# Seven-product stage of a decoder trunk: partial sums written into PSUM banks by ScalarE, no root on normed tiles, and the query rope in one piece

## The chip, the core and the metric

The kernel runs on one core of a Trainium2 chip. Its time is device microseconds for one execution. A core has five engines that work through queues of their own in program order and wait for each other by semaphores: TensorE (PE in the profile; PEld is its weight load), VectorE (DVE), ScalarE (ACT), GpSimd (POOL) and SyncE (SP). SP and POOL issue most of the DMAs here.

## The reference, cut to what matters

A trunk of two layers on a sequence of 1024 tokens with a width of 1024, all in float32. The first layer is a gated linear recurrence, which the change does not touch. The second is latent attention with 8 heads. Between them lie the projections that concern us:

```python
h = rms_norm(x_stream, norm_kv)
ckr = h @ w_dkv                                    # 256 + 64 columns
c_kv = rms_norm(ckr[..., :KV_RANK], kv_norm)
k_rope = apply_rope(ckr[..., KV_RANK:], cos[None], sin[None])
...
h = rms_norm(x, norm_g)
u = h @ w_in                                       # 384 + 1024 columns
c_q = rms_norm(u[..., :Q_RANK], q_norm)
gate = u[..., Q_RANK:]
q = jnp.einsum("bsc,chd->bshd", c_q, w_uq)
q_rope = apply_rope(q[..., QK_NOPE:], cos[None, :, None], sin[None, :, None])
o = causal_block_attention(q_nope, q_rope, k_nope, k_rope, v)
y = o.reshape(bsz, seq, N_HEADS * V_DIM) * jax.nn.silu(gate)
```

with `rms_norm(x, g) = x * rsqrt(mean(x * x) + EPS) * g`. The 256 columns of c_kv and the 384 of c_q are normed a second time; the key's rope part and the gates are not.

## The kernel before

Data is kept transposed: 128 features on the partitions, tokens along the free axis, in pages of 1024 tokens and halves of 512. A float32 product is three matmuls (`mm3`, lines 113 to 116): each factor is split into a high part (`hl`, line 82, ScalarE's copy) and a low part (line 83, VectorE's difference), and hi·hi, hi·lo and lo·hi are added up in one PSUM bank.

First come the recurrence and its output projection, which leaves x1, the residual stream, as eight tiles. Its sum of squares is collected in `acc1` (`sq_a`), and `factors` makes seven combinations of the tiles, `fx[0]` to `fx[6]`: x1 times the joined projection (14 row blocks of 128) is done in seven pairs of row blocks by a scheme of seven products in the place of eight. `pair(m, dst, w, banks, mid)` does one pair (m = 0, 2, ... 12): each product is `fmul`, 12 matmuls on one `fx[i]` and one combination of weights from `wpair`, and four banks a, c, b, d take the products. Below, "product fx3" is the one on `fx[3]`.

In `pair` before, a, c, b and d take the products fx0 to fx3. ScalarE copies a to q1 (line 607); VectorE makes v2 = b - q1, u3 = d + v2 and, after `mid`, u3 - c. Then fx4 is added onto a, fx5 onto d, fx6 onto c, and VectorE adds or subtracts v2 for two of the results. Each of the four results is multiplied by `r1`, the root of x1 (`byr`, line 162).

Pair 0 gives the two tiles of c_kv (`kvt`), pair 2 the key's rope tile and the first tile of c_q (`qt`), pair 4 the other two, and the pairs 6, 8, 10 and 12 (loop at line 743, j = 0, 2, 4, 6) the gates. `mid` puts other work between the products: in pair 0 `roots` (the root of x1: sum over the partitions by a matmul on tiles of `acc1` split in two, lines 142 to 144, then `newton`, lines 148 to 151); in pair 2 `normed` for c_kv and in pair 6 `normed` for c_q (sums by the matmuls of line 661, then `newton`, then the multiplications of line 665). After pair 6 the tiles of c_q are split; after pair 8 `qrope(0)` and after pair 10 `qrope(1)` make the queries' rope parts: 36 matmuls each, then for each half six VectorE operations (lines 733 to 735) and two splits, whose results go to DRAM. Pair 12 takes its banks from the pool of the attention stage, which opens at line 750 when the pool of the earlier banks is closed.

`wpair` loads four weight blocks (SP; line 503, tile wa), multiplies each by its gain (line 507, four pieces on ScalarE), and makes seven combinations (line 519, VectorE), each split in a wh (ScalarE) and a wl (VectorE). There are four wh and four wl buffers: the split for a product waits until an earlier product has released one. Tiles named tk come from one pool of eight.

The order of instructions on each engine is set by a scheduler when the kernel is built, from the order of the code, priorities (`tc.high_priority`, weights ahead of the rest) and the release of buffers. On the chip each queue then runs in that order.

Of the kernel before, what the change touches and what calls it, by code (L numbers as in the profile page):

```python
# [9 lines left out]
F32 = mybir.dt.float32  # L10
F32R = mybir.dt.float32r
AF = mybir.ActivationFunctionType
ALU = mybir.AluOpType
# [5 lines left out]
D = 1024  # L19
NKT = 8  # L20
NCT = 10
NH = 8
EPS = 1e-6
SCALE = 192 ** -0.5
NEG = -1e30
P = 128
# [15 lines left out]
HW = 512  # L42
# [12 lines left out]
NA, CW, CB, BR, BI, LAM, NKV, KVN, NB, QN, FN, NVEC = 0, 8, 48, 58, 68, 78, 88, 96, 98, 106, 109, 117  # L55


def trunk(tc, xT, wina, vecs, wgate, wouta, winc, wuk, wuv, wuq, wuqr, woutb, rope, outT):
    nc = tc.nc
    V, A, T, G = nc.vector, nc.scalar, nc.tensor, nc.gpsimd  # L60
# [10 lines left out]
    def nm(s):  # L71
        uid[0] += 1
        return f"{s}_{uid[0]}"

    def page(dt=F32R):
        return pgs.tile([P, S], dt, tag="pg", name=nm("pg"))
# [46 lines left out]
    def hs(h):  # L123
        return slice(h * HW, (h + 1) * HW)
# [21 lines left out]

    def newton(out, ps, inv, y, u):
        A.activation(out=y, in_=ps, func=AF.Abs_reciprocal_sqrt, scale=inv)
        V.tensor_tensor(out=u, in0=y, in1=y, op=ALU.mult)
        V.scalar_tensor_tensor(out=u, in0=ps, scalar=inv, in1=u, op0=ALU.mult, op1=ALU.mult)  # L150
        V.scalar_tensor_tensor(out=out, in0=u, scalar=-3.0, in1=y, op0=ALU.add, op1=ALU.mult)

    def sumsq(acc, sq, first, n):

        if first:
            V.scalar_tensor_tensor(out=acc, in0=acc, scalar=EPS * n / P, in1=sq, op0=ALU.add, op1=ALU.add)
        else:
            V.tensor_tensor(out=acc, in0=acc, in1=sq, op=ALU.add)

    def byr(out, src, r):  # L160

        V.scalar_tensor_tensor(out=out, in0=src, scalar=-0.5, in1=r, op0=ALU.mult, op1=ALU.mult)
# [254 lines left out]
    for ct in range(NCT):  # L417
        ps = ps0[:2] if ct == 0 else psn
# [37 lines left out]
    acc1 = rbp.tile([P, S], F32, tag="rb", bufs=1, name="acc1")  # L456
# [45 lines left out]
    def wblock(m, h, t):  # L502
        nc.sync.dma_start(out=t, in_=winc[m, :, hs(h)])
        g = gkv if m < 3 else gb
        for k in range(4):
            c = slice(k * P, (k + 1) * P)
            A.activation(out=t[:, c], in_=t[:, c], func=AF.Copy, scale=g[:, 4 * h + k:4 * h + k + 1])
        return t

    def wpair(m, new):  # L510

        def split(t):
            hi = wp.tile([P, HW], F32R, tag="wh", bufs=4, name=nm("wh"))
            lo = wp.tile([P, HW], F32R, tag="wl", bufs=4, name=nm("wl"))
            hl(t, hi, lo)
            out.append((hi, lo))

        def add(o, x, y):
            V.tensor_tensor(out=o, in0=x, in1=y, op=ALU.add)

        out = []
        with tc.high_priority(offset=WPC):
            a11, a21, a22 = wblock(m, 0, new()), wblock(m + 1, 0, new()), wblock(m + 1, 1, new())
            split(a11)
            s = wp.tile([P, HW], F32, tag="wr", bufs=2, name=nm("ws"))
            add(s, a21, a22)
            split(s)
            add(s, s, a11)
            split(s)
            add(a11, a11, a21)  # L530
            split(a11)
            a12 = wblock(m, 1, new())
            split(a12)
            split(a22)
            add(a12, a12, s)
            split(a12)
        return out

    w1 = wtile(wouta[4], NCT)
# [11 lines left out]
    for j in range(1, 3):  # L551
        x1s = []
        for dt in (j, j + 4):
            xr = residual(dt)
            w = wtile(wouta[dt], NCT)
# [21 lines left out]
    w0 = wpair(0, tt)  # L577
# [7 lines left out]
    tcp = pc.enter_context(tc.tile_pool(name="tcp", bufs=1, reuse_waits="tile"))  # L585
    r1 = acc1

    def tmp(tag, dt=F32):
        return tcp.tile([P, HW], dt, tag=tag, name=nm(tag))

    def tk(dt=F32):
        return tcp.tile([P, HW], dt, tag="t", bufs=8, name=nm("tk"))

    def fmul(ps, w, i, js, first):
        for j in js:
            c = slice(j * P, (j + 1) * P)
            hi, lo = fx[i][j // 2]
            mm3(ps, (w[0][:, c], w[1][:, c]), (hi[:, hs(j % 2)], lo[:, hs(j % 2)]), first and j == 0, j == 3, not first)

    def pair(m, dst, w, banks, mid=None):  # L600

        a, c, b, d = banks
        q1, v2, u3 = tmp("q1"), tcp.tile([P, HW], F32, tag="v2", bufs=2, name=nm("v2")), tmp("u3")
        for i, ps in enumerate((a, c, b, d)):
            fmul(ps, w[i], i, range(4), True)
            if i == 0:
                A.activation(out=q1, in_=a, func=AF.Copy)
            elif i == 2:
                V.tensor_tensor(out=v2, in0=b, in1=q1, op=ALU.subtract)
            elif i == 3:  # L610
                V.tensor_tensor(out=u3, in0=d, in1=v2, op=ALU.add)
        if mid:
            mid()
        V.tensor_tensor(out=dst[1][1], in0=u3, in1=c, op=ALU.subtract)
        byr(dst[1][1], dst[1][1], r1[:, hs(1)])
        fmul(a, w[4], 4, range(4), False)
        byr(dst[0][0], a, r1[:, hs(0)])
        fmul(d, w[5], 5, range(4), False)
        V.tensor_tensor(out=dst[1][0], in0=d, in1=v2, op=ALU.add)
        byr(dst[1][0], dst[1][0], r1[:, hs(0)])  # L620
        fmul(c, w[6], 6, range(4), False)
        V.tensor_tensor(out=dst[0][1], in0=c, in1=v2, op=ALU.subtract)
        byr(dst[0][1], dst[0][1], r1[:, hs(1)])

    def wa():
        return tcp.tile([P, HW], F32, tag="wa", bufs=NWA, name=nm("wa"))
# [1 line left out]
    def four():  # L628
        return [pst() for _ in range(4)]

    def halves(t):
        return [t[:, hs(0)], t[:, hs(1)]]

    def square(ts, acc, j):
        for h in range(2):
            if j == 0:
                A.activation(out=acc[h], in_=ts[j][:, hs(h)], func=AF.Square)
            else:
                sq = tk()
                A.activation(out=sq, in_=ts[j][:, hs(h)], func=AF.Square)  # L640
                sumsq(acc[h], sq, j == 1, P * len(ts))

    def two():
        return tk(F32R), tk(F32R)
# [9 lines left out]
    def normed(ts, acc, ps_, gcol, fac):  # L654
        n = len(ts)
        gs = con.tile([P, n], F32, name=nm("gs"))
        V.tensor_scalar(out=gs, in0=vec[:, gcol:gcol + n], scalar1=-0.5 * fac, scalar2=None, op0=ALU.mult)
        for h in range(2):
            ps = pst()
            for i in range(2):  # L660
                T.matmul(out=ps, lhsT=onesr, rhs=ps_[h][i], start=i == 0, stop=i == 1)
            newton(acc[h], ps, 1.0 / (P * n), tk(), tk())
            for j in range(n):
                t = ts[j][:, hs(h)]
                V.scalar_tensor_tensor(out=t, in0=t, scalar=gs[:, j:j + 1], in1=acc[h], op0=ALU.mult, op1=ALU.mult)

    def roots():
        for h in range(2):
            rstd(acc1[:, hs(h)], r1[:, hs(h)], pst(), 1.0 / D, tk(), tk(), two())

    kvt = [page(F32) for _ in range(2)]
    kvacc = [tk() for _ in range(2)]
    pair(0, [halves(t) for t in kvt], w0, four(), roots)
    for j in range(2):
        square(kvt, kvacc, j)
    kvps = presum(kvacc)
    krt = page(F32)
    qt = [page(F32) for _ in range(3)]
    pair(2, [halves(krt), halves(qt[0])], wpair(2, wa), four(), lambda: normed(kvt, kvacc, kvps, KVN, 1.0))
    qacc = [tk() for _ in range(2)]  # L680
    square(qt, qacc, 0)


# [24 lines left out]
    for j in range(4):  # L708
        i = j ^ 1
        DQ.dma_start(out=krs[32 * j:32 * j + 32, :], in_=krt[32 * i:32 * i + 32, :])  # L710
    pair(4, [halves(qt[1]), halves(qt[2])], wpair(4, wa), four())
    for j in range(1, 3):
        square(qt, qacc, j)
    qps = presum(qacc)
# [28 lines left out]
    for j in range(0, NH, 2):  # L743
        gts = [[tk(), tk()] for _ in range(2)]
        w = wpair(6 + j, wa)
        if j < NH - 2:
            banks = four()
        else:

            pp.close()  # L750
            pss = es.enter_context(tc.tile_pool(name="pss", bufs=2, space=PSUM, reuse_waits="tile"))
            banks = [pss.tile([P, HW], F32, tag="pm", bufs=4, name=nm("pm")) for _ in range(4)]
        pair(6 + j, gts, w, banks, None if j else lambda: normed(qt, qacc, qps, QN, SCALE))
        for i in range(2):
            for h in range(2):
                A.activation(out=gts[i][h], in_=gts[i][h], func=AF.Silu)
                DQ.dma_start(out=gd[j + i, :, hs(h)], in_=gts[i][h])
        if j == 0:
            cq = []
            for t in qt:  # L760
                cq.append((page(), page()))
                for h in range(2):
                    hl(t[:, hs(h)], cq[-1][0][:, hs(h)], cq[-1][1][:, hs(h)])
            cs, sn = tables()
        elif j < NH - 2:
            qrope(j // 2 - 1)

    def pm():
        return pss.tile([P, HW], F32, tag="pm", bufs=4, name=nm("pm"))
# [323 lines left out]
```

## Time and profile before

| | |
|---|---|
| median of 3 runs | 898.17 us (896.16 to 898.38) |
| the profiled execution | 899.38 us, of which the span from first to last instruction is 897.6 |
| mean granted TensorE clock | 0.986 |
| busy in the span | TensorE 865.4, VectorE 685.1, ScalarE 498.6, GpSimd 80.3 us |
| seven-product stage | from 371.0 us (first product of pair 0), with the last pair from 519.4 us |

In a row of waits stands who waited, at which line and for which tile, for whom, with the sum, the number and the longest in us. A row of a timeline has the start, the duration (matmuls overlap, so the distance between two starts is their pace), the engine, the line, the operation, and in brackets the idle time ahead of it and what ended it. The granted clock is 1.00 when TensorE runs at full speed.

### The profile page before, as it was taken

To read this page: it belongs to the slowest core of one execution; us is meant where nothing else is said; L and a number is where in the kernel's file an instruction comes from. 1 tells how busy PE (TensorE), PEld (TensorE's weight loads), DVE (VectorE), ACT (ScalarE), POOL (GpSimd) and SP (SyncE) were. 2 spreads that over 40 slices of the span, in tenths; PEclk is the share of its full clock that TensorE was granted. 3 is DMA by queue.
4 is the path that set the end of the run, shared out by engine and by line. 5 is a ranking of instruction groups with operands and counts; after the bars stand their busy time and mean duration, and the time that the engine had idled before them with its cause. 6 is when DMAs were issued, how large, how long until landed. Compare 5 with 4: busy or idle time off the path is not lost. (4 is left out here: it accounts for less than half of the span.)

```text
span 897.6 us, 12180 instructions
## 1 busy us (share of the span) xinstructions
PE 865.4 (96%) x4326; PEld 732.8 (82%) x4326; DVE 685.1 (76%) x1260; ACT 498.6 (56%) x915; POOL 80.3 (9%) x147
## 2 busy tenths in 40 slices
PE   7999999999999999999999788999999999999995
PEld 5788888888887888878778567989989998888995
DVE  7888788777877754899999945878978887875453
ACT  6357776777787434596675324655655554431112
POOL 2111100111000100001211220000000000010000
PEclk9999999999999999999999989999999999999998
DMA  7333333333212544133435465222223235756032
GB/s 246 120 95 96 93 103 98 100 105 95 71 47 84 169 141 147 48 107 123 168 124 184 147 233 148 68 79 89 89 74 110 71 106 192 254 199 223 8 138 68
DMA packets 51789, 109.00 MB, mean 121 GB/s; under 512 B 6544, under 2 KB 16656, under 8 KB 51728
## 3 DMA queue, kind: packets, MB, share of 16 engines
q1 hardware_dynamic: 36240, 67.45, 23.4%
q0 software_dynamic: 15216, 40.51, 13.5%
q8 instruction: 34, 0.56, 0.3%
q10 hardware_dynamic: 272, 0.26, 0.1%
q14 instruction: 27, 0.22, 0.1%
HBM read 81.46 MB, written 26.21 MB: 120 GB/s over the span
## 5 line engine op out<-in xcount | busy, mean ns | idle before, releaser
L115 PE MATMUL ps<-pg,wh 128*128 128x512 f32 x672 | 262.5, 392 | 3.4 <-DVE pg L262 3.3
L114 PE MATMUL ps<-pg,wh 128*128 128x512 f32 x672 | 262.5, 393 | 1.9 <-ACT wh L82 1.1
L116 PE MATMUL ps<-pg,wl 128*128 128x512 f32 x672 | 262.3, 391 | 0.1
L115 PEld LDWEIGHTS ps<-pg,wh 128*128 128x128 f32 x672 | 126.9, 189 | 31.6 <-DVE pg L262 4.4
L114 PEld LDWEIGHTS ps<-pg,wh 128*128 128x128 f32 x672 | 126.5, 189 | 30.3 <-ACT wh L82 2.3
L116 PEld LDWEIGHTS ps<-pg,wl 128*128 128x128 f32 x672 | 126.8, 189 | 27.3 <-DVE wl L83 1.4
L82 ACT ACTIVATE pt<-pm 128x512 fp32r<-128x512 f32 (+2 forms) x96 | 44.4, 490 | 59.7 <-PE pm L856 56.0
L846 ACT ACTIVATE pg<-s,m 128x128 f32<-128x128 f32 (+3 forms) x64 | 47.5, 742 | 44.6 <-DVE m L843 39.8
L114 PE MATMUL pm<-pg,pg 128*128 128x256 f32 (+1 forms) x192 | 61.9, 322 | 0.0
L115 PE MATMUL pm<-pg,pg 128*128 128x256 f32 (+1 forms) x192 | 61.6, 321 | 0.0
L116 PE MATMUL pm<-pg,pg 128*128 128x256 f32 (+1 forms) x192 | 61.3, 319 | 0.0
L114 PE MATMUL pm<-pg,wh 128*128 128x512 f32 x108 | 43.4, 402 | 9.9 <-DVE tk L734 9.9
L83 DVE TENSOR_TENSOR pt<-pm,pt 128x512 fp32r<-128x512 f32 (+2 forms) x96 | 50.5, 547 | 1.9 <-ACT pt L82 1.8
L843 DVE TENSOR_REDUCE m<-s 128x1 f32<-128x128 f32 (+3 forms) x64 | 48.1, 753 | 1.0
L358 DVE SCALAR_TENSOR_TENSOR t<-xb,vec,t 128x512 f32<-128x512 f32 x60 | 44.7, 746 | 0.4
L82 ACT ACTIVATE wh<-wr 128x512 fp32r<-128x512 f32 (+2 forms) x57 | 30.7, 543 | 24.3 <-PE ps L115 11.7
L116 PE MATMUL pm<-pg,wl 128*128 128x512 f32 x108 | 43.3, 401 | 0.0
L115 PE MATMUL pm<-pg,wh 128*128 128x512 f32 x108 | 43.3, 401 | 0.0
L856 PE MATMUL pm<-ident,pg 128*128 128x128 f32 x288 | 42.4, 274 | 0.3 <-DVE pg L848 0.3
L82 ACT ACTIVATE pg<-pg 128x512 fp32r<-128x512 f32 x42 | 26.2, 630 | 29.4 <-DVE pg L412 17.8
L83 DVE TENSOR_TENSOR wl<-wr,wh 128x512 fp32r<-128x512 f32 (+2 forms) x57 | 32.9, 578 | 12.2 <-ACT wh L82 11.3
L836 PE MATMUL s<-pg,pg 128*128 128x512 f32 (+2 forms) x96 | 37.5, 391 | 3.3 <-ACT pg L846 3.3
(231 smaller groups left out, 1805.7 us busy)
## 6 DMA issues: line engine op xcount, KB each, us to landing
wr<-wina SPq DMA_DIRECT2D x40, 256.0 KB, 2.8
wh<-wina POOLq DMA_DIRECT2D x36, 256.0 KB, 2.9
wa<-winc SPq DMA_DIRECT2D x24, 256.0 KB, 2.7
ysd<-pg POOLq DMA_DIRECT2D x12, 512.0 KB, 3.2
pg<-ysd SPq DMA_DIRECT2D x12, 512.0 KB, 8.3
wr<-wouta SPq DMA_DIRECT2D x16, 256.0 KB, 2.7
t<-xT SPq DMA_DIRECT2D x16, 256.0 KB, 3.8
x1d<-t POOLq DMA_DIRECT2D x16, 256.0 KB, 3.2
```

The lines of the kernel that those rows point to most:

```text
L82: A.activation(out=hi, in_=src, func=AF.Copy)
L83: V.tensor_tensor(out=lo, in0=src, in1=f(hi), op=ALU.subtract)
L114: T.matmul(out=ps, lhsT=w[0], rhs=r[0], start=first, stop=False, skip_group_check=more)
L115: T.matmul(out=ps, lhsT=w[0], rhs=r[1], start=False, stop=False, skip_group_check=more)
L116: T.matmul(out=ps, lhsT=w[1], rhs=r[0], start=False, stop=last, skip_group_check=more)
L358: V.scalar_tensor_tensor(out=xc, in0=xb[:, j:j + HW], scalar=cwv[j], in1=xc, op0=ALU.mult, op1=ALU.add)
L836: T.matmul(out=sc[:, c], lhsT=q[0][:, ql], rhs=k[0][:, c], start=True, stop=False)
L843: V.tensor_reduce(out=m, in_=sc, axis=AX.X, op=ALU.max, negate=True)
L846: A.activation(out=p_[:, 0:nk], in_=sc, func=AF.Exp, bias=m, accum_out=l)
L856: T.transpose(out=ps[:, (b - b0) * P:(b - b0 + 1) * P], in_=p_[:, b * P:(b + 1) * P], identity=ident)
```

## The change

It has five parts.

1. In `pair`, ScalarE writes -a into bank b, and product fx2 is added onto it, so b holds v2 at once. Product fx4 goes onto a directly after that. ScalarE then copies b to bank d, and product fx3 is added onto it, so d holds u3; v2 is also copied to SBUF, and c to a tile cc. Then come `mid`, d - cc, product fx6 onto c (less v2), and product fx5 onto d, which needs no addition any more. ScalarE copies four banks in a pair, where it copied one; VectorE has lost three of the operations between banks.
2. Tiles that are normed later (both of pair 0, the second of pair 2, both of pair 4) are not multiplied by r1 (`raw`); ScalarE copies those that need no subtraction. So that the second norm comes out as in the reference, its sum of squares starts from `eps`: `acc1` times a small factor, four ScalarE copies taken before `roots` overwrites `acc1`. All squares are then added on VectorE. The four eps tiles come from the pool of tk, which now has nine.
3. In `newton`, y squared is made by ScalarE (Square) and no longer by VectorE.
4. `wpair` makes the plain a12 fourth and the combinations in the order of the products.
5. Both `qrope` follow pair 8 (j = 2).

```diff
     def newton(out, ps, inv, y, u):
         A.activation(out=y, in_=ps, func=AF.Abs_reciprocal_sqrt, scale=inv)
-        V.tensor_tensor(out=u, in0=y, in1=y, op=ALU.mult)
+        A.activation(out=u, in_=y, func=AF.Square)
...
+            a12 = wblock(m, 1, new())
+            split(a12)
             add(a11, a11, a21)
             split(a11)
-            a12 = wblock(m, 1, new())
+            add(a12, a12, s)
             split(a12)
             split(a22)
-            add(a12, a12, s)
-            split(a12)
...
-        return tcp.tile([P, HW], dt, tag="t", bufs=8, name=nm("tk"))
+        return tcp.tile([P, HW], dt, tag="t", bufs=9, name=nm("tk"))
...
+        fmul(a, w[0], 0, True)
+        A.activation(out=b, in_=a, func=AF.Copy, scale=-1.0)
+        fmul(c, w[1], 1, True)
+        cc = tcp.tile([P, HW], F32, tag="cc", bufs=2, name=nm("cc"))
+        A.activation(out=cc, in_=c, func=AF.Copy)
+        fmul(b, w[2], 2, False)
+        fmul(a, w[3], 4, False)
+        A.activation(out=d, in_=b, func=AF.Copy)
+        v2 = tcp.tile([P, HW], F32, tag="v2", name=nm("v2"))
+        A.activation(out=v2, in_=b, func=AF.Copy)
+        fmul(d, w[4], 3, False)
         if mid:
             mid()
...
+        def put(i, h, src):
+            if raw[i]:
+                A.activation(out=dst[i][h], in_=src, func=AF.Copy)
+            else:
+                byr(dst[i][h], src, r1[:, hs(h)])
+
+        def put2(i, h, x, y):
+            V.tensor_tensor(out=dst[i][h], in0=x, in1=y, op=ALU.subtract)
+            if not raw[i]:
+                byr(dst[i][h], dst[i][h], r1[:, hs(h)])
+
+        put2(1, 1, d, cc)
+        put(0, 0, a)
+        fmul(c, w[5], 6, False)
+        put2(0, 1, c, v2)
+        fmul(d, w[6], 5, False)
+        put(1, 0, d)
...
+            sq = tk()
+            A.activation(out=sq, in_=ts[j][:, hs(h)], func=AF.Square)
+            sumsq(acc[h], sq, False, 0)
+
+    def eps(n):
+
+        out = [tk() for _ in range(2)]
+        for h in range(2):
+            A.activation(out=out[h], in_=acc1[:, hs(h)], func=AF.Copy, scale=EPS * n / D)
+        return out
...
+    kvacc, qacc = eps(2 * P), eps(3 * P)
...
-        elif j < NH - 2:
-            qrope(j // 2 - 1)
+        elif j == 2:
+            for g in range(2):
+                qrope(g)
```

Three places of the new order matter below.

First, ScalarE between pair 0 and pair 2, from the high part of the first half of acc1 (first row) on; the high part of the second half is the other row that reads acc. Before:

```order
L82 ACTIVATE tk_3341<-acc_2418 128x512
L148 ACT_TABLE_LOAD
L148 ACTIVATE tk_3339<-ps_3338 128x512
L507 ACTIVATE wa_3427<-wa_3427,vec 128x128 x4
L507 ACTIVATE wa_3433<-wa_3433,vec 128x128 x4
L507 ACTIVATE wa_3439<-wa_3439,vec 128x128 x4
L82 ACTIVATE wh_3445<-wa_3427 128x512
L507 ACTIVATE wa_3465<-wa_3465,vec 128x128 x3
L82 ACTIVATE wh_3451<-ws_3449 128x512
L507 ACTIVATE wa_3465<-wa_3465,vec 128x128
L82 ACTIVATE tk_3354<-acc_2418 128x512
```

Now:

```order
L82 ACTIVATE tk_3359<-acc_2418 128x512
L82 ACTIVATE wh_3463<-ws_3456 128x512
L82 ACTIVATE wh_3473<-wa_3467 128x512
L617 ACTIVATE pg_3284<-ps_3286 128x512
L617 ACTIVATE pg_3285<-ps_3289 128x512
L507 ACTIVATE wa_3659<-wa_3659,vec 128x128 x4
L148 ACT_TABLE_LOAD
L148 ACTIVATE tk_3357<-ps_3356 128x512
L507 ACTIVATE wa_3665<-wa_3665,vec 128x128
L149 ACTIVATE tk_3358<-tk_3357 128x512
L82 ACTIVATE tk_3372<-acc_2418 128x512
```

Before, the first high part stood ahead of three wa blocks of four pieces, and the second ten rows behind it. Now those three blocks (12 pieces) have moved ahead of the first high part, behind cc, and with them two splits, four pieces of a fourth block and the copy of v2; between the two high parts stand two more splits, the two raw copies of pair 0's results, four pieces, and the first root's table load, root and Square with a piece between.

Second, VectorE at the end of the rope. Before, from the last use of a rope bank (ps_4559) to the first work for the last pair:

```order
L734 TENSOR_TENSOR tk_4590<-ps_4559,pg_4064 128x512
L735 TENSOR_TENSOR tk_4589<-tk_4589,tk_4590 128x512
L83 TENSOR_TENSOR tk_4595<-tk_4589,tk_4594 128x512
L83 TENSOR_TENSOR wl_4649<-wa_4642,wh_4648 128x512
L519 TENSOR_TENSOR wa_4642<-wa_4642,ws_4626 128x512
```

Now, from the rope's last bank pair (ps_4390, ps_4391) on; ps_4496 is bank d of pair 10, and the row with cc is its d - cc:

```order
L744 TENSOR_TENSOR tk_4421<-ps_4390,pg_4068 128x512
L745 TENSOR_TENSOR tk_4422<-ps_4391,pg_4067 128x512
L519 TENSOR_TENSOR ws_4627<-ws_4627,wa_4605 128x512
L746 TENSOR_TENSOR tk_4421<-tk_4421,tk_4422 128x512
L519 TENSOR_TENSOR wa_4605<-wa_4605,wa_4611 128x512
L83 TENSOR_TENSOR wl_4635<-ws_4627,wh_4634 128x512
L83 TENSOR_TENSOR tk_4427<-tk_4421,tk_4426 128x512
L622 TENSOR_TENSOR tk_4435<-ps_4496,cc_4522 128x512
L162 SCALAR_TENSOR_TENSOR tk_4432<-ps_4493,acc_2418 128x512
```

The rope's rows stood after pair 10's results; now they stand ahead of them.

Third, TensorE at pair 8, where ps_3914 and ps_3918 are bank d of pair 6 in its product fx5. Before, one product of pair 8 and one matmul of the next stand ahead of it:

```order
L115 MATMUL ps_4129<-pg_2970,wh_4090 128x512
L116 MATMUL ps_4129<-pg_2969,wl_4091 128x512
L114 MATMUL ps_4130<-pg_2541,wh_4096 128x512
L114 MATMUL ps_3914<-pg_2563,wh_3902 128x512
L115 MATMUL ps_3914<-pg_2564,wh_3902 128x512
L116 MATMUL ps_3914<-pg_2563,wl_3903 128x512
```

Now three products of pair 8 do (on ps_4132, ps_4133 and ps_4134; the last matmuls of the third are shown):

```order
L114 MATMUL ps_4134<-pg_2981,wh_4104 128x512
L115 MATMUL ps_4134<-pg_2982,wh_4104 128x512
L116 MATMUL ps_4134<-pg_2981,wl_4105 128x512
L114 MATMUL ps_3918<-pg_2563,wh_3911 128x512
L115 MATMUL ps_3918<-pg_2564,wh_3911 128x512
L116 MATMUL ps_3918<-pg_2563,wl_3912 128x512
```

Product fx5 of pair 6 has moved back by almost two products.

More of the change, by code (lines that the diff above doesn't have):

```diff
@@ L586, in trunk, with fmul @@
     r1 = acc1
-    def tmp(tag, dt=F32):
-        return tcp.tile([P, HW], dt, tag=tag, name=nm(tag))
     def tk(dt=F32):
-        return tcp.tile([P, HW], dt, tag="t", bufs=8, name=nm("tk"))
-    def fmul(ps, w, i, js, first):
-        for j in js:
+        return tcp.tile([P, HW], dt, tag="t", bufs=9, name=nm("tk"))
+    def fmul(ps, w, i, first):
+        for j in range(4):
             c = slice(j * P, (j + 1) * P)
@@ L598, in fmul, with pair @@
             mm3(ps, (w[0][:, c], w[1][:, c]), (hi[:, hs(j % 2)], lo[:, hs(j % 2)]), first and j == 0, j == 3, not first)
-    def pair(m, dst, w, banks, mid=None):
+    def pair(m, dst, w, banks, raw=(False, False), mid=None):
         a, c, b, d = banks
[L603 to L611, printed above, removed]
+        fmul(a, w[0], 0, True)
[9 more added lines that the diff above has]
+        fmul(d, w[4], 3, False)
         if mid:
             mid()
[L614 to L623, printed above, removed]
+        def put(i, h, src):
[13 more added lines that the diff above has]
+        put(1, 0, d)
     def wa():
@@ L635, in square @@
         for h in range(2):
[L636 to L641, printed above, removed]
+            sq = tk()
[6 more added lines that the diff above has]
+        return out
     def two():
@@ L669, in roots @@
             rstd(acc1[:, hs(h)], r1[:, hs(h)], pst(), 1.0 / D, tk(), tk(), two())
+    kvacc, qacc = eps(2 * P), eps(3 * P)
     kvt = [page(F32) for _ in range(2)]
-    kvacc = [tk() for _ in range(2)]
-    pair(0, [halves(t) for t in kvt], w0, four(), roots)
+    pair(0, [halves(t) for t in kvt], w0, four(), (True, True), roots)
     for j in range(2):
@@ L678, in trunk @@
     qt = [page(F32) for _ in range(3)]
-    pair(2, [halves(krt), halves(qt[0])], wpair(2, wa), four(), lambda: normed(kvt, kvacc, kvps, KVN, 1.0))
-    qacc = [tk() for _ in range(2)]
+    pair(2, [halves(krt), halves(qt[0])], wpair(2, wa), four(), (False, True), lambda: normed(kvt, kvacc, kvps, KVN, 1.0))
     square(qt, qacc, 0)
@@ L710, in trunk @@
         DQ.dma_start(out=krs[32 * j:32 * j + 32, :], in_=krt[32 * i:32 * i + 32, :])
-    pair(4, [halves(qt[1]), halves(qt[2])], wpair(4, wa), four())
+    pair(4, [halves(qt[1]), halves(qt[2])], wpair(4, wa), four(), (True, True))
     for j in range(1, 3):
@@ L752, in trunk @@
             banks = [pss.tile([P, HW], F32, tag="pm", bufs=4, name=nm("pm")) for _ in range(4)]
-        pair(6 + j, gts, w, banks, None if j else lambda: normed(qt, qacc, qps, QN, SCALE))
+        pair(6 + j, gts, w, banks, mid=None if j else lambda: normed(qt, qacc, qps, QN, SCALE))
         for i in range(2):
```

## The prediction

> **What bounds the kernel now.** I read the page first, then the waits of TensorE, then the engines by stretch, then the timelines of the stage that is changed.
>
> ```profile
> span 897.6 us, 12180 instructions
> PE 865.4 (96%) x4326; PEld 732.8 (82%) x4326; DVE 685.1 (76%) x1260; ACT 498.6 (56%) x915; POOL 80.3 (9%) x147
> ```
>
> TensorE is busy for 96% of the span, so an edit that issues the same matmuls can only touch the 32 us in which it stands. The waits of TensorE say where these are:
>
> ```profile
> PE pm L114 <- DVE tk L734: 9.9, 1, 9.9
> PE ps L143 <- ACT tk L82: 1.4, 1, 1.4
> PE ps L114 <- ACT wh L82: 1.1, 2, 0.8
> PE ps L661 <- DVE tk L83: 1.1, 2, 0.6
> ```
>
> One wait of 9.9 us stands out: the first matmul of the last pair waits for VectorE, which still works off the query rope. The stretches (columns: us, PE, PEld, DVE, ACT, POOL busy with counts, granted clock, DMA share, GB/s) show why, and what a wait costs beside itself:
>
> ```profile
> 371.00:519.40 148.40, 135.67 (x590) 109.38 (x588) 139.91 (x228) 95.79 (x213) 23.92 (x45) 0.98 0.40 136
> 519.30:524.60 5.30, 5.23 (x12) 4.18 (x13) 1.35 (x2) 0.79 (x2) 3.13 (x6) 0.50 0.86 294
> 524.60:539.00 14.40, 14.40 (x64) 11.88 (x63) 7.27 (x12) 4.84 (x9) 2.16 (x4) 0.99 0.64 222
> 552.80:555.40 2.60, 0.22 (x2) 0.01 (x1) 1.08 (x5) 1.77 (x4) 0.00 (x0) 1.00 0.70 227
> 555.40:559.20 3.80, 3.78 (x11) 3.29 (x12) 1.99 (x7) 1.76 (x7) 0.00 (x0) 0.55 0.00 0
> ```
>
> From pair 0's first product to the wait VectorE is busy for 139.91 of 148.40 us (228 instructions, 0.61 us each): in this stage it is the second bound. After the wait TensorE runs at a granted clock of 0.50, and also after 2.6 us that were almost empty (0.55).
>
> ```profile
> 371.00 0.39 PE L114 MATMUL ps<-pg,wh 128*128 128x512 f32 x1
> ...
> 382.33 0.39 PE L116 MATMUL ps<-pg,wl 128*128 128x512 f32 x1
> 382.56 0.40 PE L143 MATMUL ps<-tk,onesr 128*128 128x512 f32 x1
> ...
> 392.14 0.50 PE L143 MATMUL ps<-tk,onesr 128*128 128x512 f32 x1 [1.43 <-ACT tk L82]
> ...
> 509.10 0.39 PE L116 MATMUL ps<-pg,wl 128*128 128x512 f32 x1
> 519.37 0.77 PE L114 MATMUL pm<-pg,wh 128*128 128x512 f32 x1 [9.88 <-DVE tk L734]
> ...
> 525.02 0.40 PE L115 MATMUL pm<-pg,wh 128*128 128x512 f32 x1
> ```
>
> Between 371.00 and 382.33 lie 50 steps: a matmul starts every 0.2266 us, a product (12) takes 2.72 us, a pair (84) 19.03 us. From 519.37 to 525.02 are 13 steps, 5.65 us where 13 at full clock take 2.95. So the wait costs 9.9 + 2.7 = 12.6 us, and that is the largest sum that the change can win.
>
> **The roots (between pairs 0 and 2).** The second root's sum is a matmul on tk, the high part of acc1, which ScalarE makes. Before, ScalarE does so at 391.48:
>
> ```profile
> 383.96 1.28 ACT L148 ACT_TABLE_LOAD   x1 [1.77 <-PE ps L144]
> 385.25 0.60 ACT L148 ACTIVATE tk<-ps 128x512 f32<-128x512 f32 x1
> 385.75 3.61 ACT L507 ACTIVATE wa<-wa,vec 128x128 f32<-128x128 f32 x12
> 389.26 0.62 ACT L82 ACTIVATE wh<-wa 128x512 fp32r<-128x512 f32 x1
> 389.79 0.97 ACT L507 ACTIVATE wa<-wa,vec 128x128 f32<-128x128 f32 x3
> ...
> 391.48 0.61 ACT L82 ACTIVATE tk<-acc 128x512 fp32r<-128x512 f32 x1
> ```
>
> These rows give ScalarE's pace in a queue that does not wait: 0.29 us for a piece of L507, 0.52 for a 512-column copy, 0.50 for L148, 1.28 for a table load. In the new order (front, first place) that tk stands behind more work. The sum of squares ends at 382.1:
>
> ```profile
> 380.83 1.28 DVE L158 TENSOR_TENSOR acc<-acc,t 128x512 f32<-128x512 f32 x2
> 382.19 32.49 SPq L503 DMA_DIRECT2D wa<-winc  x12
> wa<-winc SPq DMA_DIRECT2D x24, 256.0 KB, 2.7
> ```
>
> The first eps copy can go before that end; the other three and cc (4 x 0.52) take ScalarE to 384.3; the first wa block lands at 382.2 + 2.7 = 384.9. From there, without a pause: 20 pieces of L507 and one more (21 x 0.29 = 6.1), four weight splits, v2, the first tk and two raw copies (8 x 0.51 = 4.1), the table load, L148, the Square that waits for L148's result (0.62) and tk (0.62): 6.1 + 4.1 + 1.28 + 0.50 + 0.62 + 0.62 = 13.2. So tk is there at 384.9 + 13.2 = 398.1, where TensorE took it up at 392.1: **+6.0 us**. TensorE is done with pair 0 at 371.0 + 19.0 = 390.0 and has the first root's two matmuls to do in the meantime, at about 391.7 and 394.6, when the first tk and its lo part come. If the DMA does not hold ScalarE it is 5.4; two more block waits would make it 7.
>
> Does the clock drop there? The two matmuls cut this wait into pieces of 1.7, 2.9 and 3.5 us. After 2.6 us almost empty it did drop (0.55 above), so I add 2.0 of the 2.7 us (part lies beside ScalarE's first copy into a bank); 0 below, 2.7 above. The Trainium skill (TensorE: Matmul & The Clock Gate, section "What's actually happening") has the clock halved after an idle window of about 3.4 us; by that page the 2.0 would hang on the last piece alone, and without it the sum would be 2.0 lower. The row at 555.40 disagrees with that window, and the row decides.
>
> **ScalarE between the products.** b = -a and d = b must be written within one product (2.72 us) after a and b end. No row shows ScalarE writing a bank; the nearest read one, or neither:
>
> ```profile
> L607 ACT ACTIVATE q<-ps 128x512 f32<-128x512 f32 x6 | 3.5, 583 | 1.5 <-PE ps L116 1.5
> L640 ACT ACTIVATE tk<-pg 128x512 f32<-128x512 f32 x6 | 3.5, 620 | 1.8 <-DVE pg L162 1.8
> ACT wa L507 <- DMA wa<-winc: 4.1, 5, 1.5
> ```
>
> I take 0.58 to 0.62 us. With a weight split ahead of it (0.52) the copy is done 1.2 us after its source, so it is hidden by 1.5 us. The cover fails where ScalarE stands before a wa block: five times before, up to 1.5 us, which cost nothing then and would now hold TensorE. I take 0.7 once (pair 4), 0 to 5 over the six pairs. A second place is the product fx5 of pair 6, moved behind three products of pair 8 (front, third place): counted from normed's sums, TensorE is there after four products, 10.9 us; the difference that frees its bank stands behind ScalarE's root and Square (2.4 with the splits ahead of them) and sixteen instructions of VectorE (counted in the new order; 16 x 0.61 = 9.8) and ends with its own 0.7: 12.9, so 2.0 late (0 to 4). Third, 0.4 for the lo part of the second sum. Removed are the waits of L661 (1.1) and 0.3 of L114: together 0.7 + 2.0 + 0.4 - 1.4 = **+1.7 us** (-1.4 to +6).
>
> **The rope.** Now 72 rope matmuls (16.3 us) stand in one row after pair 8, and the last pair has none ahead of it: the 12.6 us go. What is late next? Call the first rope matmul Q. VectorE's share of the rope now ends inside pair 10 (front, second place). Product fx5 there starts at Q + 16.3 + 6 x 2.72 = Q + 32.6, and it needs the bank that the difference d - cc reads, which stands 33 instructions (counted in the new order) behind the third weight's lo part; that waits for ScalarE's split, which waits for the buffer of the third rope weight, free when the 63rd rope matmul ends, Q + 14.4. So lo at Q + 15.6, the difference 33 x 0.61 = 20.1 later, plus its own 0.7. Beside these are four hand-overs of the kind
>
> ```profile
> 513.98 0.69 DVE L83 TENSOR_TENSOR tk<-tk,tk 128x512 fp32r<-128x512 f32 x1 [0.74 <-ACT tk L82]
> ```
>
> of which part is covered (1.2 together): Q + 37.6, and TensorE stands 5.0 us (3.8 without hand-overs, 6 with all of them). That again drops the clock, 2.4 (0 to 2.7). **7.4 - 12.6 = -5.2 us.**
>
> **Edits with one answer.** VectorE loses 31 operations of the pairs and the u = y*y of six roots, and gains four sums: 33 x 0.61 = 20 us less in the stage. It shortens the stage only where VectorE is last, which is counted above. The last root stays as it was: a Square on ScalarE in the place of
>
> ```profile
> 888.42 0.38 ACT L148 ACTIVATE t<-pm 128x256 f32<-128x256 f32 x1 [0.25 <-PE pm L1024]
> 888.84 0.43 DVE L149 TENSOR_TENSOR t<-t 128x256 f32<-128x256 f32 x1 [1.65 <-ACT t L148]
> ```
>
> is about 0.38 for 0.43 us: nothing (-0.1 to +0.2). The first root of the kernel lies beside matmuls that do not stand there. The other order of the weights changes which split waits, and is in the rows above.
>
> **Sum.** 6.0 + 2.0 + 1.7 - 5.2 = +4.5 us. The profiled execution takes 899.4 us (span 897.6 and 1.8 around it), so 903.9; it lies 1.2 above the median of the runs, 898.2, so the forecast for a median is 902.7.
>
> **The rivals.**
> Forecast, 45%: the stage gives back more at the roots than it wins at the rope, 901 to 906.
> Faster, 22%: the new waits come out at their lower ends, and the wait at the last pair goes whole. The place is TensorE's second root sum: with ScalarE there 5.4 us later and no drop of the clock, nothing on the way (-1.4), and 3.8 us at product fx5 of pair 10 with the clock up, the sum is 5.4 - 1.4 + 3.8 - 12.6 = -4.8, that is 893.4. It decides where the four new costs (6.0, 2.0, 1.7 and 7.4, together 17.1) stay under 12.6 - 2.7 = 9.9. For it speaks the 20 us that VectorE loses, against it the count of instructions ahead of tk.
> No difference, 23%: the roots' wait, cut into pieces, leaves the clock up, and the two small pauses (0.7 and 2.0) are covered: 4.5 - 2.0 - 2.7 = -0.2, that is 898.0. Against it the row at 555.40, for it that the fx5 pause rests on one count. The window of the Trainium skill's page (TensorE: Matmul & The Clock Gate) is on this rival's side.
> Slower still, 10%: ScalarE is late with a bank in most pairs, because it now carries three more copies a pair and stands before the wa blocks: six times 0.7 more, 4.5 + 4.2 = 8.7, that is 906.9. Against it: 95.79 us busy of 148.40, so it catches up.
>
> **How the numbers follow.** A measurement of this kernel tells 0.3% (2.7 us) from no change. The likeliest case gives 902.7. Its own range is 900 to 906. The range reaches down to the faster rival's value and up to the slower one's, 893.5 to 907.5, and leaves out half of each outer case. Slower by over 0.3%: 0.45 + 0.10 less the part of the forecast's case that ends under 900.9, 0.03: 0.52; within: 0.23 + 0.03 = 0.26; faster: 0.22.
>
> **What would show it.** Right: the second L143 starts near 398 and waits for ACT tk; no wait at the last pair's first matmul; a wait of about 5 us ahead of product fx5 in pair 10, ended by the difference L622; the clock near 0.5 after both. The forecast is wrong if the second L143 starts before 395 or product fx5 of pair 10 waits under 3 us. Waits of L114 for ACT ps of over 1 us in several pairs would speak for the slowest rival.

## The result, and the profile after

The changed kernel takes 903.5 us (median of 4 runs, 902.38 to 904.24), the kernel before, beside it, 898.27 (896.16 to 898.56). The ratio is 1.0062 with a 95% interval of 1.0043 to 1.0081, so it is slower by 5.6 us. The profiled execution takes 904.24.

```profile
span 902.5 us, 12189 instructions
...
PE 866.3 (96%) x4326; PEld 732.3 (81%) x4326; DVE 663.0 (73%) x1222; ACT 519.5 (58%) x956; POOL 80.0 (9%) x147
```

VectorE has lost 22 us of work, ScalarE has gained 21, and the span is 4.9 us longer. The waits of TensorE in the changed kernel (who waits <- whom: us, times, longest); L602 is b = -a, L608 d = b, L622 the differences in `put2`:

```profile
PE ps L114 <- DVE tk L622: 6.7, 2, 5.2
PE ps L143 <- ACT tk L82: 4.5, 2, 3.0
...
PE ps L114 <- ACT ps L608: 2.4, 3, 1.5
PE ps L114 <- ACT ps L602: 2.1, 1, 2.1
PE ps L144 <- DVE tk L83: 2.1, 1, 2.1
```

The wait of 9.9 us for L734 has gone. In its place stand two: one for the roots and one for a difference. TensorE's timeline shows where (start, duration; in brackets the idle time ahead and what ended it):

```profile
391.17 0.50 PE L143 MATMUL ps<-tk,onesr 128*128 128x512 f32 x1 [1.47 <-ACT tk L82]
393.78 0.79 PE L144 MATMUL ps<-tk,onesr 128*128 128x512 f32 x1 [2.11 <-DVE tk L83]
397.58 0.79 PE L143 MATMUL ps<-tk,onesr 128*128 128x512 f32 x1 [3.00 <-ACT tk L82]
...
403.71 0.43 PE L114 MATMUL ps<-pg,wh 128*128 128x512 f32 x1
...
448.41 0.50 PE L114 MATMUL ps<-pg,wh 128*128 128x512 f32 x1 [2.12 <-ACT ps L602]
...
471.23 0.50 PE L114 MATMUL ps<-pg,wh 128*128 128x512 f32 x1 [1.51 <-DVE tk L622]
...
513.80 0.50 PE L114 MATMUL ps<-pg,wh 128*128 128x512 f32 x1 [1.45 <-ACT ps L608]
...
519.15 0.39 PE L116 MATMUL ps<-pg,wl 128*128 128x512 f32 x1
524.69 0.79 PE L114 MATMUL ps<-pg,wh 128*128 128x512 f32 x1 [5.15 <-DVE tk L622]
...
529.97 0.44 PE L114 MATMUL pm<-pg,wh 128*128 128x512 f32 x1
...
561.97 0.44 PE L848 MATMUL s<-pg,pg 128*128 128x384 f32 x1 [1.07 <-ACT pg L858]
```

The first three rows are the roots, in three pieces, and from 393.78 on a matmul takes 0.79 or 0.63 us: the clock is down until 403.71. The row at 524.69 is product fx5 of pair 10. The last pair starts at 529.97 with no wait. What holds the second root is read from ScalarE's timeline, what holds fx5 from VectorE's:

```profile
394.31 1.28 ACT L148 ACT_TABLE_LOAD   x1
395.60 0.60 ACT L148 ACTIVATE tk<-ps 128x512 f32<-128x512 f32 x1
...
396.39 0.62 ACT L149 ACTIVATE tk<-tk 128x512 f32<-128x512 f32 x1
396.91 0.62 ACT L82 ACTIVATE tk<-acc 128x512 fp32r<-128x512 f32 x1
```

```profile
523.95 0.69 DVE L622 TENSOR_TENSOR tk<-ps,cc 128x512 f32<-128x512 f32 x1
```

The second tk (396.91) stands behind the table load, L148 and the Square, and d - cc is done at 524.64, as the matmul behind it starts.

The stage can be summed by counting. From the first matmul of pair 0 to the first of the last pair TensorE issues 588 matmuls (6 pairs of 84, 4 of the roots, 8 of `normed`, 72 of the rope), 133.2 us at a pace of 0.2266. Before, these take 371.00 to 519.37, so 15.1 us are lost; after, 370.48 to 529.97, so 26.3. Where:

| us lost against that pace | before | after |
|---|---|---|
| the roots, with the clock | 1.7 | 10.5 |
| last pair (before) or pair 10 (after), with the clock | 12.7 | 7.9 |
| all else between the products | 3.4 | 7.8 |
| start of the attention, with the clock | 3.9 | 1.2 |

That is 8.8 - 4.8 + 4.4 - 2.7 = +5.7; the stage starts 0.5 earlier, and the spans differ by 4.9.

### The profile page after: what moved, and what is told of

Its sections match the earlier page's. It is cut to its first block, busy times and chain, and to the rows that moved or that the text cites. A ratio compares the mean times of both kernels' runs of the same rounds, so it can differ in the third digit from the quotient of the medians.

```text
span 902.5 us, 12189 instructions
## 1 busy us (share of the span) xinstructions
PE 866.3 (96%) x4326; PEld 732.3 (81%) x4326; DVE 663.0 (73%) x1222; ACT 519.5 (58%) x956; POOL 80.0 (9%) x147
## 4 chain that ended last, share of the span: by engine, by line
PE 58%; issue 16%; DVE 12%; ACT 6%; DMA 4%; POOL 2%; SPq 0%; POOLq 0%; DVEq 0%; ACTq 0%
PE pm L116 6%; PE pm L115 6%; PE pm L114 6%; PE ps L115 6%; PE ps L114 6%; PE ps L116 6%; PE pm L868 3%; PE pm L884 2%; PE pm L885 2%; PE s L849 2%; PE s L850 2%; PE s L848 2%; PE s L852 2%; PE s L851 2%; PE pm L883 2%
## 5 line engine op out<-in xcount | busy, mean ns | idle before, releaser
L82 ACT ACTIVATE pg<-pg 128x512 fp32r<-128x512 f32 x42 | 26.3, 631 | 31.9 <-DVE pg L412 17.9
L115 PE MATMUL pm<-pg,wh 128*128 128x512 f32 x108 | 42.3, 392 | 0.0
L114 PE MATMUL pm<-pg,wh 128*128 128x512 f32 x108 | 42.2, 391 | 0.0
```

The costliest lines, as they stand in the source:

```text
L82: A.activation(out=hi, in_=src, func=AF.Copy)
L114: T.matmul(out=ps, lhsT=w[0], rhs=r[0], start=first, stop=False, skip_group_check=more)
L115: T.matmul(out=ps, lhsT=w[0], rhs=r[1], start=False, stop=False, skip_group_check=more)
```

## The experiments

Every ratio below is to the kernel before, from runs on the same chip. In the three groups of experiments the kernel before took 897.25, 896.91 and 897.87 us, so runs of different groups are compared by their ratios.

### Undo one part, or do one alone

**Both roots' splits together** (the changed kernel, roots alone edited):

```diff
-        for h in range(2):
-            rstd(acc1[:, hs(h)], r1[:, hs(h)], pst(), 1.0 / D, tk(), tk(), two())
+        parts = []
+        with tc.high_priority(offset=30):
+            for h in range(2):
+                parts.append(two())
+                hl(acc1[:, hs(h)], *parts[h])
+        for h in range(2):
+            ps = pst()
+            T.matmul(out=ps, lhsT=onesr, rhs=parts[h][0], start=True, stop=False)
+            T.matmul(out=ps, lhsT=onesr, rhs=parts[h][1], start=False, stop=True)
+            newton(r1[:, hs(h)], ps, 1.0 / D, tk(), tk())
```

> The changed kernel with one edit: both splits of the first root's sum of squares (ScalarE's copy tk and VectorE's lo part) are issued together, ahead of the table load, so that the second tk no longer stands behind L148, the Square and a wa piece. Theory (ScalarE's queue ahead of the second tk makes the roots' wait, 10.5 us with the clock drop): the second root's first sum starts near 392.6 instead of 397.6, the three pauses come to some 3 us with no clock drop, and the time falls by 6 to 8 us, to 896 to 898. Rival (ScalarE and the weight blocks' DMA are what the whole stage waits for, so what is won at the roots is lost again at the next copies into banks): the pauses at pairs 2 to 10 grow by most of it and the time stays at 901 to 904.

Measured: 897.9 us, ratio 1.0004 (0.9989 to 1.0019). TensorE at the roots (L687 and L688 are the two matmuls of a sum):

```profile
389.49 0.51 PE L687 MATMUL ps<-tk,onesr 128*128 128x512 f32 x1 [0.98 <-ACT tk L82]
390.87 0.50 PE L688 MATMUL ps<-tk,onesr 128*128 128x512 f32 x1 [0.88 <-DVE tk L83]
391.53 0.50 PE L687 MATMUL ps<-tk,onesr 128*128 128x512 f32 x1 [0.17 <-ACT tk L82]
```

The second root starts at 391.53 instead of 397.58 (1.2 us of this because pair 0 ends so much earlier), no matmul is slow behind it, and 2.8 us are lost here instead of 10.5. The time falls by 5.2 us (1.0062 to 1.0004), a little less than the 6 to 8 of the theory; its runs lie between 895.28 and 900.51 (mean granted clock 0.993 to 0.987), and the profile is that of the fastest. The rival (all of it lost again) is out: ScalarE's queue ahead of the second tk made the roots' loss.

**The rope in two pieces again** (the changed kernel without part 5):

```diff
-        elif j == 2:
-            for g in range(2):
-                qrope(g)
+        elif j < NH - 2:
+            qrope(j // 2 - 1)
```

> The changed kernel with part 5 undone: the second half of the query rope is again made after pair 10. Theory (the rope in one piece is worth what the prediction's sum says): the wait in pair 10 goes, and the last pair's first matmul waits about 9 us for VectorE's last rope product (18 instructions of 0.61 and four hand-overs after the first 18 rope matmuls), 11.7 with the clock drop, against 7.9 lost in pair 10 now: 3 to 5 us slower, 906.5 to 908.5. Rival (VectorE has lost 20 us of work in the stage, and this alone would have taken the old wait away): the last pair waits under 5 us and the time is 899 to 903.

Measured: 900.19 us, ratio 1.0028 (1.0017 to 1.0039): 3 us faster than with part 5, where the theory had 3 to 5 slower. TensorE and ScalarE at the last pair (L602 is b = -a, L746 the sum in the rope):

```profile
529.05 0.80 PE L114 MATMUL pm<-pg,wh 128*128 128x512 f32 x1 [4.90 <-ACT pm L602]
```

```profile
527.37 0.63 ACT L82 ACTIVATE tk<-tk 128x512 fp32r<-128x512 f32 x1 [2.73 <-DVE tk L746]
527.90 0.61 ACT L82 ACTIVATE wh<-wa 128x512 fp32r<-128x512 f32 x1
528.42 0.58 ACT L602 ACTIVATE pm<-pm 128x512 f32<-128x512 f32 x1
```

The rival holds: the wait of 9.9 us is 4.9 without part 5. Its nature has changed too. The last pair's first product no longer waits; it is ScalarE's copy into bank b that is late, and it stands in ScalarE's queue behind a split of the rope that waits 2.73 us for VectorE.

**The rope in one piece alone** (the kernel before with the same edit the other way round).

> The kernel before with part 5 alone: both halves of the query rope follow pair 8. Theory (in the kernel before VectorE is busy for 94% of the stage, so moving its work can move the wait but not remove it): the wait of 9.9 us at the last pair goes, but pauses of about the same sum come up inside pair 10 for VectorE's sums, and the time is within 4 us of before, 895 to 899. Rival (the rope in one piece is worth 5 us or more by itself, whatever VectorE's load): 889 to 893.

Measured: 898.14 us, ratio 1.0009 (0.9996 to 1.0022). L614 is the difference u3 - c:

```profile
518.09 0.77 PE L114 MATMUL ps<-pg,wh 128*128 128x512 f32 x1 [9.62 <-DVE tk L614]
```

The pause is as long as before, in pair 10 and no longer at the last pair. With VectorE busy throughout, moving its work moved the wait and won nothing, as the theory had it.

**Parts 1 and 4 alone** (the kernel before with the new `pair` and `wpair`; L605 is b = -a here):

```diff
+        fmul(a, w[0], 0, True)
+        A.activation(out=b, in_=a, func=AF.Copy, scale=-1.0)
...
+        fmul(b, w[2], 2, False)
+        fmul(a, w[3], 4, False)
+        A.activation(out=d, in_=b, func=AF.Copy)
```

> The kernel before with parts 1 and 4 alone: partial sums in the banks by ScalarE and the order of the weights; all tiles are still multiplied by x1's root, no eps copies, y squared on VectorE, rope split as before. Theory (the roots' loss comes from the queue ahead of the second tk, which here holds no raw copies, no Square and four wa pieces less): the second root's first sum starts near 394, a loss there of 2 to 4 us instead of 10.5; pauses of 0.7 to 2 us for ScalarE's copies into banks in two to four pairs, 3 to 5 us together; the last pair waits 8 to 10 us for VectorE. Together 899 to 904. Rival (the copies into banks themselves cost the time, and the roots' loss is theirs): the second root's first sum is as late as in the changed kernel, 397 or later, and the time is 905 or more.

Measured: 895.02 us, ratio 0.9977 (0.9964 to 0.9990): 2 us faster than before, better than both theories.

```profile
391.39 0.50 PE L143 MATMUL ps<-tk,onesr 128*128 128x512 f32 x1 [1.15 <-ACT tk L82]
...
524.02 0.80 PE L114 MATMUL pm<-pg,wh 128*128 128x512 f32 x1 [5.16 <-ACT pm L605]
```

The second root starts at 391.39, earlier than the 392.14 of before, and the last pair waits 5.16 us where it waited 9.88. So the partial sums in the banks and the order of the weights are a gain; the roots' loss belongs to parts 2 and 3.

### The pause in pair 10, and part 2

**The difference in place** (the changed kernel; of its pairs those of the gates):

```diff
-        put2(1, 1, d, cc)
+        if raw[1]:
+            put2(1, 1, d, cc)
+        else:
+            with tc.high_priority(offset=0):
+                V.tensor_tensor(out=cc, in0=d, in1=cc, op=ALU.subtract)
+            byr(dst[1][1], cc, r1[:, hs(1)])
```

> The changed kernel with one edit: the difference d - cc of the gate pairs is written onto cc itself and no longer into a new tile tk, so that it need not wait for a tk that the rope still holds, and stands nine instructions earlier in VectorE's queue in pair 10 (in pair 6 three of normed's stand no longer ahead of it). Theory (the pause in pair 10 is the place of this difference behind the rope in VectorE's queue): nine instructions of 0.61 are 5.5 us, so the 5.15 us at product fx5 of pair 10 go to under 0.7, with no clock drop there, and the time falls by 5 to 8 us, to 895.5 to 898.5 where the changed kernel has 903.5. Rival (the rope's work has to be done before the last pair anyway): a pause of 4 us or more comes up at the last pair, where ScalarE's copy into the bank or the bank itself waits for the rope, and the time stays at 900 to 904.

Measured: 902.42 us, ratio 1.0059 (1.0043 to 1.0074), no faster than the change within the intervals. The pause in pair 10 has gone, as the theory said, but others have come: one at the last pair, as the rival said but shorter than its 4 us, and one in pair 8 that neither theory had named:

```profile
477.33 0.98 PE L114 MATMUL ps<-pg,wh 128*128 128x512 f32 x2 [1.79 <-ACT wh L82]
...
532.36 0.50 PE L114 MATMUL pm<-pg,wh 128*128 128x512 f32 x1 [2.61 <-ACT pm L602]
```

Behind each of these the clock drops. Both wait for ScalarE. The scheduler also put product fx5 of pair 6 ahead of pair 8, so the edit did not stay local. The edit also has two sides, the new target and the priority block around the line; in all runs here they come together.

**The early splits and the difference in place** (both edits).

> The changed kernel with both edits, the early second split at the roots and the difference d - cc written onto cc. Theory (the two pauses are separate, at the two ends of the stage): both gains add up, 5 to 6 us of the first and 5 to 8 of the second: 890 to 893.5. Rival (ScalarE, VectorE or the blocks of weights set the end of the stage, so the second gain is lost once the first is had): 896 to 899.

Measured: 898.88 us, ratio 1.0023 (1.0005 to 1.0040). The gains do not add up: the second is lost as before, again with a pause for a split in pair 8 (3.13 us) and one at the last pair (2.57 us). The theory is out, and the rival's time is right.

**Parts 1, 4 and 5 and the difference in place** (no raw tiles, no eps, y squared on VectorE; the difference is in place in all pairs).

> The kernel before with parts 1, 4 and 5 and the difference d - cc written onto cc; no raw tiles, no eps copies, y squared on VectorE. Theory (parts 1 and 4 win by VectorE's relief, and what is left at the last pair, 5.16 us and the clock drop behind it, is the rope's order): with the rope in one piece and the difference in place there is no pause over 2 us after pair 8, and the time falls from 895 by 5 to 7 us, to 888 to 890.5. Rival (the pause comes up again at the difference in pair 10 or at the last pair, as it did when the rope alone was moved): 893 to 897.

Measured: 889.67 us, ratio 0.9919 (0.9902 to 0.9935): the best of all, 7.3 us faster than before. The last pair in this kernel, and the stage (us, PE, PEld, DVE, ACT, POOL busy, clock, DMA share, GB/s):

```profile
516.79 0.47 PE L114 MATMUL pm<-pg,wh 128*128 128x512 f32 x1 [1.97 <-DVE tk L162]
```

```profile
371.00:519.40 148.40, 141.09 (x608) 112.91 (x607) 129.65 (x210) 103.47 (x232) 24.85 (x48) 1.00 0.42 146
```

There is no pause over 2 us after pair 8 and the clock stays at 1.00. Over the whole span VectorE has more work here (671.5 us) than in the changed kernel (663.0), and this kernel is 13 us faster by the ratios: the amount of VectorE's work does not decide between the two.

**Parts 1, 2 and 4** (the changed kernel with y squared on VectorE and the rope in two pieces).

> The kernel before with parts 1, 2 and 4 (the changed kernel with y squared on VectorE and the rope in two pieces again). Theory (part 2 makes the roots' loss: its raw copies, its eps copies and the four tk that they hold keep the second tk back): the second root's first sum starts at 396.5 to 397.5 and the time is 898.5 to 900.5, near the 900.2 with the Square on ScalarE. Rival (the Square on ScalarE, which waits for L148 with the second tk behind it, makes it): that sum starts before 394 and the time is 894.5 to 896.5, as with parts 1 and 4 alone.

Measured: 902.13 us, ratio 1.0053 (1.0035 to 1.0070).

```profile
397.92 0.80 PE L143 MATMUL ps<-tk,onesr 128*128 128x512 f32 x1 [2.77 <-ACT tk L82]
```

Against parts 1 and 4 alone (0.9977) part 2 costs 6.8 us, and the second root is as late as in the whole change with no Square in the queue. The rival is out; the theory has the place right, and its time is 1.6 us too low. With the Square on ScalarE the same kernel had 1.0028, so part 3 won some 2 us here (the two intervals just overlap).

### Why part 2 costs, and what part 5 is worth

**The eps tiles in pages** (the changed kernel; they hold no tk, since `n == n` always holds):

```diff
     def eps(n):
-        out = [tk() for _ in range(2)]
+        out = halves(page(F32)) if n == n else [tk() for _ in range(2)]
```

> The changed kernel with one edit: the four eps tiles lie in two pages and no longer in the pool of tk, so that no tk is held from the roots to the norms. The raw copies, the Square and the rope stay as in the change. Theory (part 2 loses its time because its eps tiles hold four of the nine tk, and so the first root's tiles and the second tk are made late): the second root's first sum starts near 392 as in the kernel before, the loss at the roots is 1 to 3 us instead of 10.5, and the time is 895 to 898. Rival (the raw copies and the Square in ScalarE's queue are enough to make it late): that sum starts at 396 or later and the time is 901 or more.

Measured: 900.95 us, ratio 1.0038 (1.0025 to 1.0051). TensorE and ScalarE here, and ScalarE with parts 1 and 4 alone (L652 are the eps copies, L613 is v2):

```profile
394.40 0.50 PE L143 MATMUL ps<-tk,onesr 128*128 128x512 f32 x1 [3.40 <-ACT tk L82]
```

```profile
380.65 2.36 ACT L652 ACTIVATE pg<-acc 128x512 f32<-128x512 f32 x4 [0.41 <-DVE acc L158]
...
383.87 0.63 ACT L82 ACTIVATE tk<-acc 128x512 fp32r<-128x512 f32 x1
```

```profile
380.52 0.57 ACT L613 ACTIVATE v<-ps 128x512 f32<-128x512 f32 x1
380.99 0.63 ACT L82 ACTIVATE tk<-acc 128x512 fp32r<-128x512 f32 x1
```

Neither theory is right. The time is 2.2 us under that of the change, with intervals that overlap, and the second root starts in the middle between 391.39 (parts 1 and 4 alone) and 397.58 (the change). Half of the delay, 3.0 us, is left: the first tk is 2.88 us later, and the eps copies (2.36 and a wait of 0.41) now stand ahead of it; there is a Square ahead of the second. The other half, 3.2 us, went with the four held tk: without them the first tk is split before the weights, and not after them, and the raw copies come behind the second.

**The same with the difference in place.**

> The changed kernel with the eps tiles in pages and the difference d - cc written onto cc. Theory (with the roots' pause gone, the pause in pair 10 is what is left of the change's cost, and the in-place difference takes it away as it did without raw tiles): 889 to 893, no pause over 2.6 us after pair 8. Rival (ScalarE carries too many copies with raw tiles, so pauses at its copies into banks and its splits take the place of the one in pair 10, as when the difference alone was moved): 895 to 898, and a pause of 1.8 us or more for a split in pair 8.

Measured: 901.55 us, ratio 1.0047 (1.0033 to 1.0061): again nothing won, and again a pause for a split in pair 8, of 2.81 us. The rival's pause is there, its time was too low by 3.5 us.

**Parts 1, 4 and 5, the difference in a new tile.**

> The kernel before with parts 1, 4 and 5, the difference d - cc in a new tile tk as in the change. Theory (the rope in one piece loses by itself, because d - cc then stands behind all of it; it wins only with the difference in place): a pause of 4 to 6 us at product fx5 of pair 10, and a time of 896 to 899, which is 1 to 4 above parts 1 and 4 alone. Rival (the rope in one piece is the gain, and the place of the difference matters little): no pause over 2 us in pair 10, 889 to 892.

Measured: 897.86 us, ratio 1.0000 (0.9990 to 1.0010). L625 is `put2`:

```profile
518.21 0.79 PE L114 MATMUL ps<-pg,wh 128*128 128x512 f32 x1 [5.11 <-DVE tk L625]
```

The difference starts at 517.47 here, behind the rope's last rows. Written in place it runs ahead of the last of them:

```profile
508.14 0.68 DVE L633 TENSOR_TENSOR cc<-ps,cc 128x512 f32<-128x512 f32 x1
```

As in the theory: part 5 costs 2 us here, and the difference in place, one operation in each pair, is worth 7.3 (1.0000 to 0.9919).

**All but part 2, with the difference in place** (the best kernel and the Square on ScalarE).

> The kernel before with parts 1, 3, 4 and 5 and the difference d - cc in place; part 2 alone is left out of the change. Theory (the Square frees VectorE and costs ScalarE 0.6 us in a queue that has room; it was worth 2 us with raw tiles): 887.5 to 890, at or under the 889.7 without it. Rival (the Square waits for L148 with the second tk behind it, and lengthens the roots' pause): the second root's first sum 0.6 us or more later, 890 to 892.

Measured: 893.23 us, ratio 0.9950 (0.9937 to 0.9962), 2.8 us slower than without the Square. The roots are not the reason, they lose 1.9 us in place of 1.4. In the profile, which is that of the slowest of five runs, it is pair 8, with a clock drop behind the pause (L608 is cc here, L611 is d = b):

```profile
468.39 1.27 PE L114 MATMUL ps<-pg,wh 128*128 128x512 f32 x2 [3.91 <-ACT wh L82]
```

```profile
465.75 2.17 ACT L82 ACTIVATE pg<-pg 128x512 fp32r<-128x512 f32 x4
467.83 0.51 ACT L82 ACTIVATE wh<-wr 128x384 fp32r<-128x384 f32 x1
468.24 0.57 ACT L608 ACTIVATE cc<-ps 128x512 f32<-128x512 f32 x1
468.72 0.58 ACT L611 ACTIVATE ps<-ps 128x512 f32<-128x512 f32 x1
```

Four splits of c_q and one of a rope weight, whose end is what TensorE's next matmul waits for, stand ahead of the copies that pair 8 needs; without the Square the pause in pair 8 is 1.46 us, and four of the splits stand behind these copies. The rival had the sign, for another reason. Why the Square makes the scheduler put them there was not tried.

## Why the prediction was right, and where it was not

The sign and the two main places were right. The time (902.7 for 903.5) is nearer than the steps deserve. By its steps:

- **The roots.** Forecast +6.0 and 2.0 for the clock; measured +8.8. The second L143 starts at 397.58 (forecast 398.1) and stands behind what the count named. The early splits show the cause: with that place in the queue gone, 5.2 us of the loss go.
- **The clock at the roots.** It drops between 391.17 and 393.78, ahead of the longest piece: pauses of 1.47 and 2.11 with one matmul between did it. The prediction had followed the row at 555.40 here, against the Trainium skill's window (TensorE: Matmul & The Clock Gate, "What's actually happening"), by which only the last piece could have brought the drop; the trace bears the row out.
- **ScalarE between the products.** Forecast +1.7, at most 6; measured +4.4. The pause at fx5 of pair 6 is 1.51 (forecast 2.0), and pair 4 loses 0.5 (forecast 0.7). The number of late copies was too low: 2.12 at 448.41 in pair 6 and 1.45 at 513.80 in pair 10 were not in the sum. Such copies in several pairs were the sign that it gave for its slowest rival.
- **The rope: right in size, wrong in its cause.** Forecast -5.2, measured -4.8, and the pause at fx5 of pair 10 is 5.15 for 5.0. But the step "the last pair has none ahead of it: the 12.6 us go" gave part 5 what other parts do anyway: with parts 1 and 4 alone the wait there is 5.16 and no longer 9.88. In the change with the rope in two pieces the last pair loses 7.7 us, no longer 12.7, and part 5 replaces that with 7.9 and more late copies: by the ratios it costs 2 to 3 us. The text did say that 20 us go from VectorE, and counted them only where VectorE was last; the wait that was being priced was just such a place.
- **The start of the attention.** Not in the sum: its wait is 1.07 and no longer 2.40, with no slow matmul behind it, 2.7 us. It goes with the new `pair` in nearly all runs (2.40 again in one of them, and in the one that moved the rope alone). Why was not tried.
- **The sum** was 0.3 us low for the profiled execution (903.9 for 904.2) because +0.8 at the roots, +2.7 between the products and +0.4 at the rope stand against -2.7 at the attention and -0.5 at the start (the rest of the span is 0.3 shorter). So the nearness is luck: the 2.7 us too few for the copies and the 2.7 us that the attention's start gave back, which the sum did not have, cancel.
- **What each part does**, by the ratios: parts 1 and 4 win 2 us, part 2 costs 6.8, part 3 wins 2 with raw tiles and costs 2.8 in the best kernel, part 5 costs 2 to 3. Part 5 and the difference in place together win 5.2 over parts 1 and 4 alone (0.9977 to 0.9919); the difference in place with the rope in two pieces was not run, so how much of this needs part 5 is open. Parts 1 and 4 were not run apart either.

## What to carry to other kernels

When a change has several parts, price each one against the state that the others leave, not against the profile of before: here one part was credited with a wait that two others had already halved. An engine that is far from saturated still sets the pace if its queue runs in order and something that waits, or a copy nobody needs yet, stands ahead of what TensorE needs next, so count places in that queue and not its busy share. A result written onto its own operand needs no buffer from a pool, and its place in the order may be worth more than the work that was saved.

## What the runs showed of the hardware

A copy by ScalarE into a PSUM bank takes what a copy out of one takes: 577 ns (L602, bank to bank), 579 (L605, bank to SBUF), six of each in the changed kernel.

The same pause gives either clock. In the changed kernel 2.12 us without a matmul at pair 6 leave it at 1.00; in the kernel with the difference in place 1.99 us at the same place halve it for the next 3.5 us. The two stretches of each, pause and what follows, first the changed kernel:

```profile
446.20:448.40 2.20, 0.09 (x1) 0.00 (x0) 2.20 (x5) 2.20 (x7) 0.00 (x0) 1.00 0.01 4
448.40:451.80 3.40, 3.39 (x15) 2.78 (x16) 3.28 (x6) 2.85 (x6) 0.58 (x1) 1.00 0.29 81
```

```profile
446.20:448.20 2.00, 0.02 (x1) 0.00 (x0) 2.00 (x5) 2.00 (x6) 0.00 (x0) 1.00 0.02 4
448.20:451.70 3.50, 3.49 (x8) 2.73 (x9) 3.37 (x6) 2.95 (x6) 0.58 (x1) 0.52 0.27 80
```

What decides is where a pause falls in a grid of time. In each of the 14 traces the granted clock changes only at multiples of 3.413 us from one another: in the changed kernel it is 1.00 for 382.29 us (112 times 3.413), 0.50 for 10.24 (3 times), 1.00 for 119.47 (35 times) and 0.50 for 6.83 (twice). Cut along this grid (from 13 to 880 us, ends of matmuls modelled), TensorE was busy for 0 to 50% of the window ahead of each of the 40 drops, and for 46% or more of every window at 1.00 that no drop followed. In the two cases above it is 46% of the window from 444.73 (changed kernel, no drop) and 42% of the one from 444.91 (difference in place, drop). A window at 0.50 was followed by 1.00 where TensorE was busy for 83% of it or more, and by another at 0.50 up to 82%.

So a drop lasts one or more whole windows, and the same pause can bring one or not: 1.77 us did, where the rope alone was moved (at 390.84), and 2.95 us did not, in the kernel with parts 1, 4 and 5 (at 17.05). A pause of 3.1 us or more in the seven-product stage always had slow matmuls behind it. The Trainium skill (TensorE: Matmul & The Clock Gate, "What's actually happening") has windows of about 3.4 us that run freely. The grid agrees, but a drop after 1.99 us disagrees with the rule there that a window must be idle: here about half of one was enough.
